# Two woven instruction streams in a two-layer hybrid encoder on eight cores

## The chip, the cores and the metric

The kernel runs on all 8 cores of one Trainium2 chip. Every core works alone on 4 of the 32 sequences. The metric is the device time of the slowest core, in microseconds.

The profiles name a core's engines: PE is the matmul array and PEld its weight loads, ACT computes activation functions, DVE and POOL work element by element, SP only issues transfers here. PSUM banks are the accumulators that matmuls write to and ACT and DVE read.

The chip has a second, slower state: in some executions the four cores of one die, or of both, run longer at a lower granted clock of the matmul array (PE). In a fast execution the granted clock is 1.00 or 0.50 and hardly anything else. In a slow one long stretches stand at 0.81: one slow die of the changed kernel had 6,955 us of them, a slow die of another version 15,086 us of 18,272. The die beside it may have none. So besides whole fast runs I compare **undisturbed dies**: the median span of the four cores of a die which shows the highest clock that this kernel reached. These medians repeat within 0.3%, across chips too. (The kernel before varies a little more: 18.10 to 18.19 ms.)

## The reference, cut to what matters

```python
# x: (32, 2048, 1024) float32; two layers; c modulates each norm per sequence
h = modulate(rms_norm(x, norm_ffn1[l]), sh1, sc1)
x = x + 0.5 * g1 * swiglu(h, ffn1_w_gu[l], ffn1_w_down[l])      # 1024 -> 2*2816 -> 1024
h = modulate(rms_norm(x, norm_mix[l]), sh2, sc2)
x = x + g2 * token_mix(h, ...)    # A: dense attention, 6 heads, rotary; B: window of +-128;
                                  # C: latent attention, 4 heads; gates, merge, projection
h = modulate(rms_norm(x, norm_ffn2[l]), sh3, sc3)
x = x + 0.5 * g3 * swiglu(h, ffn2_w_gu[l], ffn2_w_down[l])
# ... after the last layer: rms_norm(x, final_norm)
```

## The kernel before

One sequence at a time stays on the core (`xT`, four tiles of 512 tokens), and each sub-layer runs over all four tiles before the next begins. All engines follow one program; each works through its own instructions in order.

```python
def emit_norm_tile(l, m, s, tt):
    r, rres = emit_rstd(tt)     # squares on ACT, sums on PE, then Ln and Exp on ACT
    for c in range(KC):
        # DVE: tf = x * r          ACT: hT = tf * A + B
        ...

# ffn_steps(l, which, s): two groups of two tiles
for tg in range(2):
    for wt in range(NGU):
        add(gu_job(wt), gu_comp(wt, tg), tag=...)
        if tg == 1 and wt in (1, 3):
            add_next_norm(l, m, s, [wt // 2])   # next sub-layer's norm of a finished tile
    for dc in range(KC):
        add(dn_job(dc), dn_comp(dc, tg), tag=...)
add_next_norm(l, m, s, [2, 3])
# ... merge_steps: for tile tt, after its output projection:
if tt >= 1:
    add_next_norm(l, 1, s, [tt - 1])

# attn_dense: scores -> exp on ACT (one 512-column tile each) -> PV, one or two tiles ahead
for (g, tt, kc) in its:
    pend.append((g, tt, kc, emit_S(g, tt, kc)))
    if len(pend) > la:
        emit_PV(*pend.pop(0))
```

Eight PSUM banks serve whichever stage runs. Weights come straight from the fp32 inputs, and each block serves two tiles.

The softmax here doesn't subtract the row's maximum and nothing guards it: scores larger than these inputs give would overflow.

## Time and profile before

| | before |
|---|---|
| all timed runs | 18,189 (fast); 18,506; 18,621; 18,681 us |
| profiled execution | 18,161.6 us, cores 18,074 to 18,162, clock 0.90, at most 8.5 us at 0.81 |
| PE / ACT / DVE busy | 88% / 37% / 33% |

The page of the profile: busy time of each engine, the PE clock in tenths over 40 equal slices, the chain of waits, and the costliest group, FFN's gate and up matmuls (busy us in all, mean ns | idle before them, and what ended most of it).

```profile
span 18161.6 us, 218237 instructions; the slowest of 8 cores (18073.6 to 18161.6 us)
## 1 busy us (share of the span) xinstructions
PE 15968.4 (88%) x68808; PEld 6725.1 (37%) x68808; DVE 6000.9 (33%) x7933; ACT 6760.2 (37%) x12620; POOL 3347.6 (18%) x4221
...
PEclk9888999889898899888989889988998989999799
...
## 4 chain that ended last, share of the span: by engine, by line
PE 76%; ACT 8%; issue 6%; DVE 4%; DMA 3%; POOL 2%; ACTq 0%; DVEq 0%; POOLq 0%; SPq 0%
...
L468 PE MATMUL bank<-hT,wslot 128*128 128x512 bf16 x22528 | 5002.9, 385 | 153.2 <-ACT tmpf L473 153.2
```

The windows view of the same run, core 3 (busy us and, in brackets, instructions; then granted clock, DMA share, GB/s), for projections, dense attention, merge and FFN:

```profile
core 3: us, PE busy (x) PEld busy (x) DVE busy (x) ACT busy (x) POOL busy (x), PEclk, DMA share, GB/s
900.00:1000.00 100.00, 59.38 (x158) 18.91 (x156) 41.23 (x62) 35.59 (x58) 0.88 (x1) 0.69 0.08 19
1100.00:1200.00 100.00, 96.06 (x384) 27.47 (x384) 48.02 (x24) 98.78 (x193) 0.00 (x0) 1.00 0.00 1
1800.00:1900.00 100.00, 83.59 (x366) 35.81 (x365) 39.58 (x61) 29.80 (x47) 54.55 (x76) 0.95 1.32 124
4400.00:4800.00 400.00, 400.00 (x1855) 181.28 (x1853) 74.51 (x106) 50.46 (x86) 63.54 (x66) 1.00 0.68 75
```

FFN needs nothing but PE: 1,855 matmuls in 400 us at clock 1.00, 215.6 ns each. Dense attention runs at ACT's pace, 384 matmuls per 100 us. In projections PE waits and its clock falls.

### The profile page before, as it was taken

How to read it: one execution, taken by the hardware profiler on the slowest of the kernel's cores; microseconds unless marked ns; L12 is line 12 of the kernel's file. 1: busy time of each engine (PE TensorE's matmuls, PEld its weight loads, DVE VectorE, ACT ScalarE, POOL GpSimd, SP SyncE). 2: the span in 40 equal slices, each digit the busy share in tenths (PEclk: the TensorE clock that was granted, in tenths of full speed). 3: DMA queues.
4: the chain of work that ended last, by engine and by line, in shares of the span. 5: the costliest groups of instructions: out<-in, count | busy, mean ns of one | idle time of the engine just before them, and what ended most of it. 6: DMA issues, size and time to landing. Idle time of an engine off the chain costs nothing.

```text
span 18161.6 us, 218237 instructions; the slowest of 8 cores (18073.6 to 18161.6 us)
## 1 busy us (share of the span) xinstructions
PE 15968.4 (88%) x68808; PEld 6725.1 (37%) x68808; DVE 6000.9 (33%) x7933; ACT 6760.2 (37%) x12620; POOL 3347.6 (18%) x4221
## 2 busy tenths in 40 slices
PE   8988899878898899888988889988898888998799
PEld 5522444223442234323443234432344323443234
DVE  1144311443224432244222442234422344223442
ACT  1164211652216522264222642146312463225531
POOL 1111311113111131112201122111311113110141
PEclk9888999889898899888989889988998989999799
DMA  5603966129561295505855058630865409652195
GB/s 111 106 11 39 114 90 72 15 33 100 89 70 17 30 103 71 60 13 59 93 86 60 12 60 91 71 45 13 87 77 88 46 13 91 72 71 28 18 105 77
DMA packets 2876904, 1137.44 MB, mean 63 GB/s; under 512 B 2012566, under 2 KB 2816284, under 8 KB 2875804
## 3 DMA queue, kind: packets, MB, share of 16 engines
q0 software_dynamic: 2829952, 1004.51, 49.9%
q1 hardware_dynamic: 45852, 118.97, 2.0%
q8 instruction: 604, 9.90, 0.2%
q14 instruction: 496, 4.06, 0.1%
HBM read 2018.45 MB, written 33.56 MB: 113 GB/s over the span
## 4 chain that ended last, share of the span: by engine, by line
PE 76%; ACT 8%; issue 6%; DVE 4%; DMA 3%; POOL 2%; ACTq 0%; DVEq 0%; POOLq 0%; SPq 0%
PE bank L468 26%; PE bank L496 14%; PE bank L717 8%; PE bank L675 5%; PE bank L705 5%; PE bank L1050 5%; DMA wslot<-w_br_c 3%; PE bank L1080 2%; PE bank L316 2%; PE bank L1059 2%; PE bank L944 2%; ACT hT L412 2%; PE bank L396 1%; PE bank L885 1%; PE bank L867 1%
## 5 line engine op out<-in xcount | busy, mean ns | idle before, releaser
L468 PE MATMUL bank<-hT,wslot 128*128 128x512 bf16 x22528 | 5002.9, 385 | 153.2 <-ACT tmpf L473 153.2
L468 PEld LDWEIGHTS bank<-hT,wslot 128*128 128x128 bf16 x22528 | 2232.0, 99 | 2900.7 <-issue 333.8
L473 ACT ACTIVATE tmpf<-bank 128x512 f32<-128x512 f32 x1408 | 836.5, 597 | 5291.8 <-PE bank L468 5291.4
L709 ACT ACTIVATE pT<-bank 128x512 bf16<-128x512 f32 x5120 | 2611.8, 601 | 81.6 <-PE bank L705 39.6
L496 PE MATMUL bank<-scr,wslot 128*128 128x512 bf16 x11264 | 2479.1, 383 | 0.0
L475 DVE TENSOR_TENSOR scr<-tmpf,bank 128x512 bf16<-128x512 f32 x1408 | 964.5, 687 | 4021.0 <-PE bank L468 3824.0
L717 PE MATMUL bank<-pT,scr 128*128 128x512 bf16 x5120 | 1945.9, 386 | 62.0 <-ACT pT L709 5.6
L496 PEld LDWEIGHTS bank<-scr,wslot 128*128 128x128 bf16 x11264 | 1113.6, 99 | 1353.4 <-issue 54.1
L742 DVE RECIPROCAL tmpf<-bank 64x512 f32<-64x512 f32 x320 | 1072.5, 3352 | 1443.4 <-PE bank L717 1439.4
L1050 PE MATMUL bank<-hT,wslot 128*128 128x512 bf16 x6144 | 1402.7, 386 | 118.1 <-DMA wslot<-w_br_c 117.0
L705 PE MATMUL bank<-scr 64*128 64x512 bf16 (+1 forms) x5120 | 1410.5, 390 | 36.7 <-DVE tmpf L663 24.6
L454 POOL DMA_DIRECT2D wslot<-ffn_w_gu x704 | 615.1, 878 | 4430.7 <-PE bank L468 3448.5
L1033 POOL DMA_DIRECT2D wslot<-w_in x768 | 673.8, 886 | 3313.4 <-PE bank L997 2097.3
L675 PE MATMUL bank<-hT,wslot 128*128 128x512 bf16 x3584 | 1002.6, 443 | 295.1 <-DVE stg L959 123.0
L500 DVE SCALAR_TENSOR_TENSOR xT<-bank,modG,xT 128x512 f32<-128x512 f32 x512 | 384.4, 751 | 2156.8 <-PE bank L496 2156.8
L717 PEld LDWEIGHTS bank<-pT,scr 128*128 128x128 bf16 x5120 | 491.1, 96 | 1524.2 <-issue 1520.0
L1053 ACT ACTIVATE tmpf<-bank 128x512 f32<-128x512 f32 x768 | 454.4, 597 | 1488.5 <-PE bank L1050 976.8
L486 POOL DMA_DIRECT2D wslot<-ffn_w_down x512 | 541.8, 1063 | 2174.2 <-PE bank L496 1079.4
L1050 PEld LDWEIGHTS bank<-hT,wslot 128*128 128x128 bf16 x6144 | 603.9, 99 | 890.0 <-issue 212.7
L1063 DVE TENSOR_TENSOR tmpf<-tmpf,bank 128x512 f32<-128x512 f32 x768 | 493.6, 684 | 1096.8 <-ACT tmpf L1053 1053.9
L675 PEld LDWEIGHTS bank<-hT,wslot 128*128 128x128 bf16 x3584 | 381.3, 109 | 873.9 <-issue 580.3
L394 ACT ACTIVATE pT<-xT 128x512 bf16<-128x512 f32 x596 | 333.0, 618 | 954.8 <-PE bank L396 523.5
(128 smaller groups left out, 13239.0 us busy)
## 6 DMA issues: line engine op xcount, KB each, us to landing
wslot<-ffn_w_gu POOLq DMA_DIRECT2D x704, 512.0 KB, 7.8
wslot<-w_in POOLq DMA_DIRECT2D x800, 256.0 KB, 7.6
wslot<-ffn_w_down POOLq DMA_DIRECT2D x512, 352.0 KB, 6.6
wslot<-ada_w POOLq DMA_DIRECT2D x72, 1024.0 KB, 6.1
wslot<-w_out POOLq DMA_DIRECT2D x64, 1024.0 KB, 12.6
scr<-x SPq DMA_DIRECT2D x64, 512.0 KB, 3.9
scr<-ropeC SPq DMA_DIRECT2D x64, 512.0 KB, 3.9
out<-scr SPq DMA_DIRECT2D x64, 512.0 KB, 2.7
```

What stands on the lines that cost most here:

```text
L454: P.op("pool", lambda E, dst=dst, src=src: E.dma_start(out=dst, in_=src), writes=[res], chan=ch)
L468: P.op("pe", lambda E, bk=bk, g=g, k=k, half=half, tt=tt: E.matmul(bk[:], lhsT=W[:, k, g, half * 128:(half + 1) * 128], rhs=hT[:, k, tt * ...
L473: P.op("act", lambda E, tf=tf, pg=pg: E.activation(out=tf[:], in_=pg[:], func=AF.Silu), reads=[pgres], writes=[tres])
L475: P.op("dve", lambda E, tf=tf, pu=pu, f=f, t2=t2: E.tensor_tensor(out=act_view(f, t2), in0=tf[:], in1=pu[:], op=ALU.mult), reads=[tres, pu ...
L496: P.op("pe", lambda E, bk=bk, f=f, t2=t2: E.matmul(bk[:], lhsT=W[:, f, :], rhs=act_view(f, t2), start=(f == 0), stop=(f == FC - 1)), reads ...
L675: P.op("pe", lambda E, k=k: E.matmul(bk[0:M, :], lhsT=W[:, k, ncolchunk], rhs=hT[:, k, tt * TT:(tt + 1) * TT], start=(k == 0), stop=(k == ...
L705: P.op("pe", lambda E, sb=sb, ka=ka, qa=qa: E.matmul(sb[:], lhsT=ka, rhs=qa, start=True, stop=True), reads=[kres, qres], writes=[sbres])
L709: P.op("act", lambda E, sb=sb, pi=pi: E.activation(out=pT[pi][:], in_=sb[:], func=AF.Exp, scale=scale), reads=[sbres], writes=[pT_res[pi]])
L717: P.op("pe", lambda E, ob=ob, va=va, pi=pi: E.matmul(ob[:], lhsT=va, rhs=pT[pi][:], start=(kc == 0), stop=(kc == S // 128 - 1)), reads=[v_ ...
L742: P.op("dve", lambda E: E.reciprocal(out=tf[dlo:dlo + 64, 0:ncols], in_=ob[dlo:dlo + 64, 0:ncols]), reads=[obres], writes=[tres])
L1033: P.op("pool", lambda E, m=m, src=src: E.dma_start(out=G[:, m, :, :], in_=src), writes=[res], chan=ch)
L1050: P.op("pe", lambda E, bk=bk, m=m, k=k: E.matmul(bk[:], lhsT=G[:, m, k, :], rhs=hT[:, k, tt * TT:(tt + 1) * TT], start=(k == 0), stop=(k = ...
```

## The change

The intent: attention leaves PE waiting for ACT, FFN leaves ACT and DVE idle, so run them together, on different sequences. The program becomes two streams: F (norms, FFN, projections; q, k, v and h go to DRAM) and M (attention, gates, merge, output projection; the residual x comes from and goes to DRAM). A planner on the host weaves them into one order. F goes tile by tile: a tile of 512 tokens passes norm, FFN, norm, (FFN, norm,) projections, then the next tile starts. PSUM is split: two banks for F, six for M. Norms, SiLU and sigmoid are rewritten so that ACT keeps one table. The diff, cut to its core:

```diff
+LAT = 0.1; DMA_LAT = 2.0; DMA_RATE = 200e3; SLACK = 0.5     # one line each in the file
+def weave(streams):
+    # ... v: how far a stream is within its phase, by PE cost
+    # ... est(o): when o could start, from planned engine and buffer times
+    while True:
+        cands = []
+        for i, st in enumerate(streams):
+            o = st.ops[heads[i]]                # only the head of each stream's one list
+            if any(n not in toks for n in o.need):
+                continue
+            cands.append((est(o), i, o))
+        mn = min(c[0] for c in cands)
+        best = min((c for c in cands if c[0] <= mn + SLACK), key=lambda c: (c[2].v, c[0]))
+        # ... run(o): plan it, append it to the order
-    banks = [nc.alloc_psum_tensor("bank%d" % i, [128, TT], F32) for i in range(8)]
+    fbank = [nc.alloc_psum_tensor("fb%d" % i, [128, TT], F32) for i in range(2)]
+    sbk = [nc.alloc_psum_tensor("sb%d" % i, [128, 2 * TT], F32) for i in range(2)]
+    obk = [nc.alloc_psum_tensor("ob%d" % i, [128, TT], F32) for i in range(2)]
-        # ... rstd: two ACT operations, Ln and Exp
+    def rsqrt_rows(st, bk, br, nr, inv_n):      # eight DVE operations, [128, 512]
+        ts(st, ms, bk[0:nr, :], inv_n, EPS, ALU.mult, ALU.add, [br], [nr_r[0]])
+        ts(st, y.bitcast(I32), ms.bitcast(I32), -0.5, MAGIC, ALU.mult, ALU.add, ...)
+        for _ in range(2):
+            stt(st, t, y, -0.5, y, ALU.mult, ALU.mult, [nr_r[1]], [nr_r[2]])
+            tt_(st, "dve", t, t, ms, ALU.mult, [nr_r[2], nr_r[0]], [nr_r[2]])
+            stt(st, y, t, 1.5, y, ALU.add, ALU.mult, [nr_r[2], nr_r[1]], [nr_r[1]])
+    def norm(l, m, s):
+        norm_stats()
+        for c in range(KC):
+            t, tr = tmp()
+            tt_(F, "dve", t[:], xc(c), nr_y[:], ALU.mult, [xF_r[c], nr_r[1]], [tr])
+            act(F, hc(c), t[:], AF.Identity, ..., scale=mA(l, m, s, c), bias=mB(l, m, s, c))
+        # ... for every tile, in F's one list:
+            fsteps.append((ph, None, first(l - 1, 2, s)))
+            fsteps += ffn_steps(ph, l - 1, 1, s, tt, None)
+            fsteps.append((ph, None, lambda s=s, l=l: norm(l, 0, s)))
+            fsteps += ffn_steps(ph, l, 0, s, tt, 2 * l)
+            fsteps.append((ph, None, lambda s=s, l=l: norm(l, 1, s)))
+            fsteps += proj_steps(ph, l, s, tt, prefetch)
+    # ... weights: first touch in fp32, a bf16 copy is stored and reloaded for every tile
+    order, t_end, busy = weave([F, M])
```

## The prediction

> **What bounds the kernel now.** The array. In the profile (18162 us) the page's first part has PE busy 88% against DVE 33%, ACT 37%, POOL 18%; the chain of waits is 76% PE. But it is three different stages, seen in the windows view of one sequence and layer (about 2.2 ms). FFN: PE 100%, 465 matmuls per 100 us at granted clock 1.00 on all eight cores, so 215 ns per 512 columns. Dense attention: ACT 99%, PE issuing only 384 per 100 us (one 512-column exp each 0.51 us sets the pace). Projections and window attention: PE 57-83% busy at clocks 0.59-0.80, waiting for DVE and ACT in turn. Merge: PE 80-93%, DMA share up to 1.32 (rows under 512 B), waiting for the branch weights.
>
> I counted the matmul columns of both programs and priced them at 215 ns per 512 (fp32 four times), 64-row pairs as one. Before: 13.6 ms of pure array time, so 4.6 ms of its 18.16 ms are gaps, lowered clock (mean 0.90) and pipeline ends.
>
> **What changes.**
> - Removed: the second pass of C projections, 1024 input transposes in fp32, the zeroing matmuls, the 2304 four-column ada matmuls; window scores become 64-row pairs. New array time 13.0 ms: only 0.6 ms less. The pairs of A already overlap before (609 us for 3072).
> - Moved: attention and merge of one sequence run inside FFN, norms and projections of another. Per 512-token tile and layer: 406 us of array, against about 205 us of ACT and 215 us of DVE (durations of before: exp 0.51 us per 512, tanh 0.6, DVE op 0.69-0.75, reciprocal 3.35). No other engine binds on average, so the gaps are what can be won.
> - Added: DVE work (two ops per FFN chunk instead of one, rsqrt as eight DVE ops, about 0.8 ms) off the critical path; DMA. Weights are reread per tile, about 61 MB per 406 us, 150 GB/s instead of 63, but in 4 KB rows from bf16 copies. Loads of 512 KB landed in 3.9 us before; with 3 and 5 slots, about 7 to 14 us ahead, this hides.
> - No table switches: Silu, Sigmoid and Ln become tanh and DVE. The Trainium skill, "ScalarE: Activation LUTs", section on table sets, puts exp and tanh in one set; before shows loads of 1.28 us.
>
> **What is left of the gaps.** FFN has only two PSUM banks: its tanh (0.6) and first DVE op (0.75), plus latency, must fit under 1.72 us of the other bank's matmuls; behind a 1 us exp they don't. Estimate: 5-9% idle in woven stretches, 0.25 ms for the first and last phases (FFN alone, norms exposed), 0.25 ms first touch of fp32 weights, 0.1 ms start; clock about 0.98. Sum: 13.0/0.98/0.93 = 14.2, plus 0.6 = 14.8 ms. Timed runs of before are 2.5% over its profile; I allow part of it inside the range.
>
> **Predicted: 14800 us, range 13900 to 16000.** Faster by over 2%: 0.97; within: 0.02; slower: 0.01.
>
> **Right if** PE is over 92% busy with ACT and DVE near 50%; mean clock at least 0.96; almost no activation table loads; matmuls per 100 us near 420-450 throughout, without stage pattern; the chain of waits over 85% PE.
>
> **Wrong if** dense matmuls on eight cores trip a limiter: the Trainium skill, "TensorE: Matmul & The Clock Gate", HAM section, gives 13/16 clock for three busy cores; this trace doesn't agree (1.00 in FFN), but longer density could, giving about 16.5 ms. Or if the fixed order, in-order engines and two FFN banks stall PE on tanh behind exp (PE under 85%, waits on fb banks), or the single SP queue blocks weight loads behind stores (PE waiting for wF or wM).

## More of the kernel before

A "call" is a session in which several kernels were timed on one chip.

What PE waited for, before (total us, times, longest):

```profile
engine line waited for: us in total, times, longest us
PE bank L396 <- ACT pT L394: 198.8, 32, 10.5
PE bank L468 <- ACT tmpf L473: 153.2, 40, 4.8
...
PE bank L1050 <- DMA wslot<-w_br_c: 117.0, 77, 4.2
PE bank L396 <- ACT sq L394: 98.7, 16, 10.3
```

The two lines of L396 are the norms (statistics waiting for squares): some 300 us in 18 ms.

## The result, and the profile after

The changed kernel took 17,155 us in the median of four runs: 16,492 and 16,517 fast, 17,792 and 17,991 slow. The ratio of the fast runs is 0.908 (95% interval 0.905 to 0.911), 9% faster. Ratios are the mean time of one kernel's fast runs over that of the other's of the same rounds, so not quite the ratio of the medians quoted. The prediction said 14,800, and 13,900 to 16,000 as its range. The direction was right; the size was not.

The page of the profiled execution:

```profile
span 16515.5 us, 199324 instructions; the slowest of 8 cores (16449.4 to 16515.5 us)
...
PE 14310.3 (87%) x63128; PEld 5831.8 (35%) x63128; DVE 6429.4 (39%) x8558; ACT 5883.1 (36%) x7980; POOL 1591.9 (10%) x1365
...
PEclk8989998999999999999999999999999999999988
...
## 4 chain that ended last, share of the span: by engine, by line
PE 74%; DVE 9%; issue 6%; ACT 6%; DMA 3%; POOL 1%; SPq 1%; DVEq 0%; ACTq 0%; POOLq 0%
...
L510 PE MATMUL fb<-hF,wF 128*128 128x512 bf16 x25600 | 6927.5, 393 | 799.2 <-ACT hF L519 428.0
```

PE is busy 87%, not over 92; its clock is 0.93, not 0.96; the chain is 74% PE (76% before). Over the whole span 63,128 matmuls are 382 per 100 us, not 420 to 450. The windows view of core 7 shows that this is no even dilution: a stretch that is really woven, one in which attention runs alone, and one that holds a norm.

```profile
core 7: us, PE busy (x) PEld busy (x) DVE busy (x) ACT busy (x) POOL busy (x), PEclk, DMA share, GB/s
5780.00:5940.00 160.00, 159.20 (x757) 66.30 (x755) 52.15 (x60) 87.49 (x104) 5.08 (x4) 1.00 0.30 96
5400.00:5480.00 80.00, 67.21 (x299) 22.07 (x297) 20.99 (x15) 72.11 (x79) 5.06 (x4) 1.00 0.02 7
4945.00:4985.00 40.00, 26.54 (x117) 10.37 (x116) 25.84 (x34) 19.46 (x25) 1.79 (x1) 0.81 0.22 76
```

The woven stretch is what the change was made for: 757 matmuls in 160 us (473 per 100 us), PE busy 99.5%, clock 1.00, ACT at 55%. The losses lie elsewhere. What PE waited for, after:

```profile
engine line waited for: us in total, times, longest us
PE fb L510 <- ACT hF L519: 605.4, 163, 24.7
PE ob L510 <- DVE pT L522: 211.2, 101, 5.6
PE fb L510 <- DVE tmpf L522: 183.8, 76, 9.7
...
PE fb L510 <- DMA wF<-wts: 37.1, 20, 8.1
```

The largest entry, 605 us, is matmuls waiting for `hF`, which holds the squares and then the normalised tile; the norms' two lines of before came to some 300. In the group lines, the gate and up matmuls (with the projections, now) have 799 us of idle time before them, 428 of it ended by `hF`; before, gate and up had 153. The other 177 of the 605 us are statistics waiting for squares. All matmul waits for weight DMA are short (37 us for the first-touch loads), though DMA moves 142 GB/s instead of 63.

One norm in the timeline of core 7 (start us, us, engine, line, operation, tiles, and in brackets the idle time before it):

```profile
start us, us, engine line op out<-in xcount [idle before <-releaser]
4962.53 0.69 DVE L533 TENSOR_SCALAR nr<-fb 128x512 f32<-128x512 f32 x1
...
4965.47 1.49 DVE L526 SCALAR_TENSOR_TENSOR nr<-nr 128x512 f32<-128x512 f32 x2
...
4968.65 4.91 DVE L522 TENSOR_TENSOR tmpf<-xF,nr 128x512 f32<-128x512 f32 x8
4969.44 5.77 ACT L519 ACTIVATE hF<-tmpf,mods,modA 128x512 bf16<-128x512 f32 x8 [8.00 <-DVE tmpf L522]
...
4970.40 4.12 PE L510 MATMUL fb<-hF,wF 128*128 128x512 bf16 x6 [8.40 <-ACT hF L519]
...
4973.47 3.35 DVE L1121 RECIPROCAL mt<-mt 128x512 f32<-128x512 f32 x1
...
4974.46 0.61 PE L510 MATMUL sb<-q,kB 64*128 64x384 bf16 x4
```

The root occupies DVE from 4962.53 to 4968.6, then the eight multiplications go to ACT one by one, and PE starts at 4970.40, 8.4 us idle, at first with one matmul per 0.7 us. M does not fill the hole: its next score matmul comes at 4974.46, and its reciprocal had to stand behind the norm's DVE operations until 4973.47. The Trainium skill, "TensorE: Matmul & The Clock Gate", section on architectural detail, says that ACT and DVE are strict first-in first-out queues; this timeline agrees. The clock in 5-us steps around the same norm:

```profile
core 7: us, PE busy (x) PEld busy (x) DVE busy (x) ACT busy (x) POOL busy (x), PEclk, DMA share, GB/s
4955.00:4960.00 5.00, 5.00 (x27) 1.94 (x25) 2.07 (x4) 3.28 (x4) 0.00 (x0) 1.00 0.51 173
...
4965.00:4970.00 5.00, 0.00 (x0) 0.00 (x0) 4.47 (x8) 0.56 (x1) 0.00 (x0) 0.50 0.00 0
4970.00:4975.00 5.00, 3.99 (x11) 0.76 (x11) 5.00 (x7) 5.00 (x8) 0.00 (x0) 0.50 0.01 2
4975.00:4980.00 5.00, 4.44 (x24) 1.81 (x22) 4.54 (x4) 2.81 (x4) 1.79 (x1) 0.86 0.09 17
```

The gap halves PE's clock, and the first matmuls after it run at half speed. The skill's same page ("What's actually happening") says an idle array falls to half clock after an idle window of about 3.4 us and recovers after a busy one. The trace agrees: its stretches of 0.50 are 3.41 us or multiples of it (but for those that the end of the span cuts), 13.65 us at this norm. In all, core 1 of after stood 2,254 of its 16,451 us at 0.50.

From the records of the traces, a span can be split into three terms: PE's busy time weighed with the granted clock (**work**), the rest of its busy time (**clock**), and its idle time. On cores without a stretch at 0.81 (sums are short by 5 to 15 us, because idle time after the last matmul is left out; the stretch before the first clock record, 168 us in before and 31 in after, is counted at 0.50, since fp32 matmuls of 128 columns start 213 ns apart there, and 109 ns apart where a record says 1.00):

| | span | work | clock | idle |
|---|---|---|---|---|
| before, core 5 | 18,150 | 14,586 | 1,378 | 2,180 |
| after, core 1 | 16,451 | 13,624 | 663 | 2,149 |
| the prediction's sum | 14,800 | 13,000 | 270 | about 1,600 |

(13.0/0.98 gives the clock term, dividing by 0.93 gives 1.0 ms of idle time, and the 0.6 ms of phases and start are counted as idle.) So the whole gain of 1.7 ms is less work, 1.0, and better clock, 0.7. **The idle time did not shrink at all**, although it is this that the weave was meant to remove. On core 7 of the profile, where every matmul record is there, 1,093 of the 2,191 us of idle time lie inside 112 norm windows (from the first statistics matmul to the eighth of F's weight matmuls after it, cut where the next window begins), 10 us each, and all windows but one hold 3 us or more. (The expectations below quote 1.24 ms from a first count; with overlaps of the windows counted twice it is 1.22.) Another 389 lie in 50 stretches of over 8 us in which only attention matmuls run.

### The profile page after: what moved, and what is told of

It reads as the page before. It is cut to its first block, busy times and chain, and to the rows that moved or that the text cites. A ratio compares the mean times of both kernels' runs of the same rounds, so it can differ in the third digit from the quotient of the medians.

```text
span 16515.5 us, 199324 instructions; the slowest of 8 cores (16449.4 to 16515.5 us)
## 1 busy us (share of the span) xinstructions
PE 14310.3 (87%) x63128; PEld 5831.8 (35%) x63128; DVE 6429.4 (39%) x8558; ACT 5883.1 (36%) x7980; POOL 1591.9 (10%) x1365
## 4 chain that ended last, share of the span: by engine, by line
PE 74%; DVE 9%; issue 6%; ACT 6%; DMA 3%; POOL 1%; SPq 1%; DVEq 0%; ACTq 0%; POOLq 0%
PE fb L510 53%; PE sb L510 12%; PE ob L510 9%; ACT pT L519 3%; DVE nr L526 2%; DVE pT L522 1%; DVE tmpf L522 1%; ACT hF L519 1%; DVE mt L1121 1%; DVE nr L522 1%; ACT mt L519 1%; DVE nr L533 1%; DMA mt<-xs 1%; SPq L543 1%; POOL tmpf L522 1%
## 5 line engine op out<-in xcount | busy, mean ns | idle before, releaser
L510 PE MATMUL fb<-hF,wF 128*128 128x512 bf16 x25600 | 6927.5, 393 | 799.2 <-ACT hF L519 428.0
L510 PEld LDWEIGHTS fb<-hF,wF 128*128 128x128 bf16 x25600 | 2478.2, 100 | 4395.3 <-issue 1877.2
L510 PE MATMUL fb<-actb,wF 128*128 128x512 bf16 x11520 | 3042.3, 383 | 50.2 <-DMA wF<-wts 17.3
L519 ACT ACTIVATE pT<-sb 128x1024 bf16<-128x1024 f32 x2560 | 2514.8, 1024 | 1293.3 <-PE sb L510 1278.9
L510 PE MATMUL ob<-pT,vv 128*128 128x512 bf16 x6176 | 1855.0, 372 | 468.0 <-DVE pT L522 211.2
L526 DVE SCALAR_TENSOR_TENSOR tmpf<-tmpf,fb 128x512 f32<-128x512 f32 x1408 | 965.8, 686 | 2727.2 <-ACT tmpf L519 2598.0
L510 PEld LDWEIGHTS fb<-actb,wF 128*128 128x128 bf16 x11520 | 1117.7, 98 | 1485.1 <-issue 210.1
L522 DVE TENSOR_TENSOR actb<-tmpf,fb 128x512 bf16<-128x512 f32 x1536 | 1056.1, 688 | 1258.8 <-PE fb L510 1034.9
L510 PE MATMUL sb<-hM,wM 128*128 128x512 bf16 x4160 | 1297.1, 388 | 30.1 <-DMA wM<-wts_bf 30.1
L1121 DVE RECIPROCAL mt<-mt 128x512 f32<-128x512 f32 x256 | 857.9, 3351 | 46.2 <-ACT mt L519 34.6
```

Source lines behind the costliest of these rows:

```text
L510: st.op("pe", lambda E: E.matmul(out, lhsT=lhsT, rhs=rhs, start=start, stop=stop, skip_group_check=True), reads=reads, writes=writes, cost ...
L519: st.op("act", lambda E: E.activation(out=out, in_=in_, func=func, **kw), reads=reads, writes=writes, cost=c_act(n))
L522: st.op(eng, lambda E: E.tensor_tensor(out=out, in0=a, in1=b, op=op), reads=reads, writes=writes, cost=c_dve(n) if eng == "dve" else c_poo ...
L526: st.op("dve", lambda E: E.scalar_tensor_tensor(out=out, in0=a, scalar=scalar, in1=b, op0=op0, op1=op1), reads=reads, writes=writes, cost= ...
L1121: M.op("dve", lambda E: E.reciprocal(out=den, in_=den), reads=[denr], writes=[denr], cost=c_rec(TT))
```

## The experiments

Theory N: the missing 1.7 ms are exposed norms, 7 per tile and 112 in all, with their idle time and the half clock behind it. Before, they hid among other tiles' matmuls. Rivals: W, the weave itself (one list for each stream, only its head a candidate, planned with assumed rates), which runs attention alone at ACT's pace; and D, the DMA traffic of 2,346 MB instead of 1,137. Times below are undisturbed dies unless another state is named; the kernel after is 16.47 ms in the same terms, and before 18.10 to 18.19.

### unwoven

```diff
-        best = min((c for c in cands if c[0] <= mn + SLACK), key=lambda c: (c[2].v, c[0]))
+        best = min(cands, key=lambda c: (c[2].phase, c[1]))    # each phase: all of F, then all of M
```

> The changed kernel with one thing undone: the two streams are not interleaved; of each phase the FFN stream is placed whole, then the attention and merge stream. Same instructions. If weaving is what the change gives (theory A), this loses all of the 1.65 ms gain and more, because norms and attention stand bare and stay in the two-bank layout: 18.3 to 19.3 ms in the fast state. If most of the gain is the smaller work (rival: fewer matmul columns, no transposes, no table switches), it stays near 17 ms.

Correct. No whole run was fast (19,580 to 20,342 us); its best dies took 18,592 to 18,609 us at clock 0.89 in four runs, inside theory A's range. Weaving is worth 2.1 ms: without it the same operations are slower than the kernel before (18,158 to 18,191 us). The rewriting alone (tiles, tanh, DRAM, split banks) gains nothing in this order.

### norm_one_op

```diff
         ms, y, t = nr_ms[0:nr, :], nr_y[0:nr, :], nr_t[0:nr, :]
+        if nr == 128:       # wrong on purpose: one operation for the eight of the root
+            ts(st, y, bk[0:nr, :], 0.0, 1.0, ALU.mult, ALU.add, [br], [nr_r[1]])
+            return
```

> Wrong output on purpose: the reciprocal root of the 128-row norms is one vector instruction in place of eight in a row. Theory N (the 112 norms are where the array idles: 1.24 of 2.19 ms idle and about 0.8 of 1.17 ms of lost clock lie in or just behind them): the chain is 5 us shorter, 112 x 5 us = 0.56 ms of idle and about half as much clock loss go, 15.6 to 15.9 ms. Rival B (FFN's two banks, tanh behind a 1 us exp) and rival P (attention run alone at ACT pace): at most 0.2 ms.

Wrong as intended (relative error 0.043). 16.01 to 16.02 ms, one whole run fast at 16,035: 0.46 ms gained, short of theory N's range by 0.1. Idle time on core 5 is 1,731 us, of it 557 in the norm windows. Seven DVE operations fewer, 5 us a norm, gave this, and the two rivals allowed 0.2. The norms matter, but the root is not all of them.

### slack0

```diff
-SLACK = 0.5
+SLACK = 0.0
```

> One constant of the scheduler: it may no longer let a stream that lags behind go first when that stalls the engine by up to 0.5 us; 0 in its place. Same instructions, other order. Theory P (attention alone for 1.13 ms at ACT pace, idle 0.39 ms in it, comes of this rule): 0.3 to 0.5 ms faster, 16.0 to 16.2 ms, and the stretches of attention alone shrink to under half. If they are there for want of ready FFN work: under 0.1 ms.

Correct, 15.90 to 15.92 ms. With slack, the planner may put the stream that lags first although its operation can start up to 0.5 us later; on an in-order queue that is a hole. Removing it gave 0.57 ms, but not where I looked for it: stretches of attention alone keep 1,103 us (1,134 after) and their idle time rises from 389 to 490 us. The norm windows keep 1,021 us of idle time. What shrank is the holes elsewhere. So the gain came out a little above the range, and the reason given for it did not hold.

### ooo

```diff
 def weave(streams):
-    # candidates: the head of each stream's list
+    # each stream has a queue per engine; the head of each queue is a candidate as soon as
+    # the ops before it that share a buffer with it are placed
+            for e, qq in q.items():
+                n, o = qq[0]
+                g = group(qq) if o.glue else [qq[0]]
+                if any(x not in done and x not in mine for _, m in g for x in deps[m]):
+                    continue
+                cands.append((est(o), o.v, i, e, len(g)))
-SLACK = 0.5
-DMA_RATE = 200e3
+SLACK = 0.0
+PE_LAT = 0.15
+DMA_RATE = 320e3
```

> Another scheduler, same instructions: each engine takes its own next instruction of a stream once those it shares a buffer with are placed, so a vector instruction at the head of the attention stream no longer keeps its later matmuls behind the norm; slack 0; DMA assumed at 320 GB/s in place of 200. If the norm's gaps are for want of placed work (theory N, second half), 15.2 to 15.7 ms, PE idle in norm windows at most half; if vector work itself is short there (rival D), at least 15.9 ms like slack0.

Correct, 15.46 to 15.48 ms, one whole run fast at 15,504: 1.0 ms less than after with the same instructions. Idle time is 1,460 us; stretches of attention alone fall to 797 us. A norm window still idles 7.5 us (844 in all), more than the half that theory N allowed. So W is a real term, as large as norm_gone will show N to be. This version changed the plan's assumptions too; list_320 separates the two.

### list_320

```diff
-DMA_RATE = 200e3
-SLACK = 0.5
+DMA_RATE = 320e3
+SLACK = 0.0
```

> Correct. The weave of the changed kernel with its slack at 0 and its assumed DMA rate at 320 instead of 200 GB/s; a stream stays one list. Separates the two things that the out-of-order version changed. If one list per stream is what costs: within 1% of slack0, 15.8-15.95 ms on an undisturbed die. If the pessimistic DMA rate in the plan is what costs: 15.4-15.6 ms, as the out-of-order version.

Correct, 15.74 to 15.75 ms. Neither expectation held: the assumed DMA rate is worth 0.16 ms and the lists the remaining 0.28. So the 1.0 ms of the planner splits into 0.57 for the slack, 0.16 for the rate, and 0.28 for one list for each stream, the last with the small changes of assumed latencies in it.

### norm_gone and ooo_norm_gone

```diff
-        act(F, hc(c), xc(c), AF.Square, [xF_r[c]], [hF_r[c]])
+        act(F, hc(c), xc(c), AF.Tanh, [xF_r[c]], [hF_r[c]])     # wrong on purpose, bounded
-        rsqrt_rows(F, bk, br, 128, 1.0 / D)
+        ts(F, nr_y[:], bk[:], 0.0, 1.0, ALU.mult, ALU.add, [br], [nr_r[1]])
     def norm(l, m, s):
         norm_stats()
-        for c in range(KC):
-            ...                 # eight multiplications on DVE, eight scalings on ACT
```

> Wrong on purpose: of each of the 112 norms only the statistics' matmuls and one DVE operation stay; the rest of the root chain (7 operations), the eight multiplications and the eight scalings are not done, and the matmuls read a bounded function of x that ACT writes where it wrote the squares. The weave is the one of the changed kernel. Theory N (the missing term is the exposed norms, idle and the clock behind it): an undisturbed die goes from 16.45-16.5 ms to 14.9-15.5 ms, PE's idle time from 2.19 ms to about 1.2 ms, mean clock from 0.93 to 0.95 or more. Rival W (the loss is in the weave, which runs attention alone at ACT's pace whatever F does): 16.0 ms or more, and the idle time only moves.

Wrong as intended (0.21). 15.50 to 15.52 ms on the better die in three runs, one whole run fast at 15,653: 0.95 ms gained, just past the upper end of theory N's range. The clock rose to 0.96 as N said, but 1,519 us of idle time stay, more than N's 1.2 ms. What PE still waits for (core 5):

```profile
engine line waited for: us in total, times, longest us
PE ob L510 <- DVE pT L522: 217.2, 104, 5.8
...
PE fb L510 <- ACT hF L519: 138.2, 54, 18.8
```

The wait for `hF` is down from 605 us on core 7 (586 on core 5) to 138 (statistics waiting for ACT's writes are among them); the waits of attention's exp and of window attention's DVE products stay. N is over half of what is missing, not all.

> Wrong on purpose, as norm_gone, with the out-of-order plan. If norms and the one-list weave are the two terms that the prediction left out, the prediction's 14.8 ms must be reached or beaten here: 14.2-14.8 ms on an undisturbed die, PE's idle time under 1.0 ms, clock 0.97 or more. If it stays over 15 ms, a third term is missing.

With the other planner and without norms: 14.74 ms, one whole run fast at 14,782. N and W held. This is the prediction's 14.8 ms, at idle time 982 us and clock 0.972; but it is a kernel that leaves work out, and its terms are not the prediction's (work 13.48 ms, not 13.0; idle 0.98, not about 1.6). That the sums meet so closely is luck; what the run shows is that the two terms are large enough. The two gains (0.95 and 1.0) overlap by 0.2. The view of all cores of its profiled run shows how a slow and an undisturbed die stand side by side:

```profile
die 0 (median of its cores): 15172.2 us, clock 0.932
die 1 (median of its cores): 14742.3 us, clock 0.972
```

### ooo_cols, cols

```diff
     def norm_stats():
         for c in range(KC):
-            mm(F, bk[:], ONE, hc(c), c == 0, c == KC - 1, ...)
+            for g in range(4):      # tokens on the partitions: sums land in [128, 4]
+                mm(F, bk[:, g:g + 1], hF[:, c * TT + g * 128:c * TT + (g + 1) * 128], ONE[:, 0:1], ..., n=1)
-        rsqrt_rows(F, bk, br, 128, 1.0 / D)
+        # the same eight DVE operations on [128, 4], split into two bf16 parts, then
+        for g in range(4):
+            for hl in range(2):     # spread over the partitions again
+                mm(F, b2[:, g * 128:(g + 1) * 128], nhl[:, hl * 4 + g:hl * 4 + g + 1].to_broadcast([128, 128]), IDB, ..., n=128)
```

> Correct. The out-of-order plan, and the norm's statistics with tokens on the partitions: 32 matmuls of one column, the eight operations of the root on 128x4 instead of 128x512, then eight matmuls of 128 columns that spread the result. Theory N: the chain from statistics to the first scaled chunk shrinks by about 3.5 us of 11, 112 times, and what it gives back is idle time at half clock: 15.1-15.3 ms on an undisturbed die (15.47 before this). Rival W: within 0.5% of 15.47 ms.

Correct, 15.32 to 15.33 ms, one whole run fast at 15,347: 0.9% faster than ooo, between the two expectations. With the better planner the root itself is worth 0.14 ms.

> Correct. The plan of the changed kernel (slack 0.5, one list for each stream), with the norm's root on 128x4 as in ooo_cols. The version with one operation in place of eight saved 0.46 ms; this one keeps all eight, small, and adds a spreading matmul: 16.0-16.25 ms on an undisturbed die. Within 0.5% of 16.47 if only the scaling operations and not the root matter.

Correct, in the changed kernel's own plan: 16.25 ms on its two undisturbed dies, 0.22 ms gained, at the weak end of the range.

### norm_not_awaited

```diff
-            mm(F, bk[:], ONE, hc(c), c == 0, c == KC - 1, [hF_r[c], const_r], [br])
+            mm(F, bk[:], ONE, hZ[:], c == 0, c == KC - 1, [const_r], [br])      # hZ: constant tile
-                    mm(F, pg[:], W[:, k, 0, :], hc(k), k == 0, k == KC - 1, [sr, hF_r[k]], [pgr])
+                    mm(F, pg[:], W[:, k, 0, :], hZ[:], k == 0, k == KC - 1, [sr, const_r], [pgr])
# the same for pu and for the A, B and C projections; every operation of the norm stays
```

> Wrong on purpose: all work of the norms is done, at the same places of the plan, but the matmuls that used its result (statistics, gate and up, A, B and C projections) read a constant tile instead. If the latency of the norm's result is the cost: 15.5-15.7 ms on an undisturbed die, as when the norms are gone. If the cost is their place in the lists and queues (the FFN's first tanh and the other stream's operations stand behind their 24 operations on ACT and DVE): 16.2 ms or more, and PE's idle time stays over 1.9 ms. I expect the second.

Wrong as intended (0.63). 16.33 to 16.34 ms on three undisturbed dies: only 0.13 ms gained, and idle time on core 5 is 2,220 us, no less than after. "The same places of the plan" holds inside F's list; the planner, which no longer sees these waits, merges M a little otherwise (58,087 of the 63,128 matmuls stand at the same place of PE's order). What PE waits for now:

```profile
engine line waited for: us in total, times, longest us
PE fb L511 <- DVE tmpf L527: 440.8, 121, 21.0
PE ob L511 <- DVE pT L523: 271.3, 105, 12.9
PE fb L511 <- ACT actb L520: 262.6, 110, 10.7
```

The 605 us that had the name `hF` moved to another name: 441 us for the FFN's first DVE operation `tmpf<-tmpf,fb`, which with the product after it frees F's two banks, 121 waits, and 263 us for ACT operations on `actb`. The page's releaser was true, and yet removing it gained almost nothing, because the FFN's own tanh and products follow the norm's 24 ACT and DVE operations in F's list and in the queues. Together with norm_gone (the same waits gone and the operations too: 0.95 ms) this shows that a norm costs by the operations that stand ahead, which wait for each other, and not by the matmuls' own wait for its result. How much of that is the order in F's list and how much the queues of ACT and DVE is not separated, and it is shown for the plan of the changed kernel only.

### half_loads

```diff
+            nl[0] += 1
+            m = n if nl[0] < 500 else n // 2      # wrong on purpose
-            dma(st, sl[:, 0:n], wb_d[l * NWJ + i][:, 0:n], [r], [res], ch, 128 * n * 2)
+            dma(st, sl[:, 0:m], wb_d[l * NWJ + i][:, 0:m], [r], [res], ch, 128 * n * 2)
```

> Wrong on purpose: the order of the changed kernel, but after the first 500 reloads of a weight block only half of its columns are fetched, which takes about a quarter of all bytes away. If the doubled DMA traffic (142 GB/s) is what ate the gain: 16.0 ms or less on an undisturbed die. If it is hidden, as the short DMA waits of PE say (about 0.15 ms in all): 16.35-16.5 ms.

Wrong as intended (0.29). The core moved 1,726 MB instead of 2,346, and took 16.445 ms in three runs, against 16.47 of the changed kernel (undisturbed dies). PE's order is that of after, matmul by matmul. D falls: the traffic is hidden.

### exp_quarter

```diff
-                    act(M, pT[p][:], sbk[i][:], AF.Exp, ..., n=1024, scale=A_SCALE)
+                    act(M, pT[p][:, 0:256], sbk[i][:, 0:256], AF.Exp, ..., n=256, scale=A_SCALE)   # wrong on purpose; C too
```

> Wrong on purpose: each exp of dense attention takes 256 of its 1024 columns, about 0.4 us in place of 1.02, 2560 times; the plan knows it. Removes ACT's pace from attention while the norms stay. Rival W (attention alone at ACT's pace, 0.39 ms of idle time): about 16.0 ms on an undisturbed die. Theory N (norms, which hold F's side whatever attention costs): at least 16.2 ms, and the idle time around the norms stays at 1.1-1.3 ms.

Wrong as intended (0.024). Two undisturbed dies, 16.128 and 16.133 ms: 0.34 ms gained, between the two expectations, so ACT's pace is a third and smaller term. (The shorter exps also leave ACT sooner to F's tanh and scalings; the run doesn't separate that.)

### after_again and best

after_again is the changed kernel, untouched.

> The changed kernel, untouched, on the same chip as the other runs of this call, so that a fast run or an undisturbed die of it stands beside theirs: 16.45-16.5 ms, clock 0.93.

16.466 to 16.475 ms on four undisturbed dies, as expected.

best is ooo_cols with M's residual tiles loaded one step earlier, and 0.25 us for the latency behind PE in the plan:

```diff
-PE_LAT = 0.15
+PE_LAT = 0.25
             def wo(q, tt=tt, hold=hold, xload=xload):
                 def fn(sl, sr):
-                    # allocate and load this step's two residual tiles
+                    xs = hold.pop(("xs", q))
+                    if q < 3:
+                        xload(q + 1, tt, hold)      # q = 0: loaded at the end of the gates
```

> Correct. The out-of-order plan, the norm's root on 128x4, and the residual tiles of the output projection loaded one step earlier (their loads take 6.6 us to land and stand in the chain of waits of the out-of-order version). 15.15-15.35 ms on an undisturbed die (15.33 without the early loads); PE's idle time no more than 1.33 ms, and the share of the residual's load in the chain of waits gone.

Correct, 15.27 to 15.30 ms, one whole run fast at 15,284. It is within its range. The residual's load did not leave the chain (1%, 2% in ooo). Its page:

```profile
span 15282.6 us, 205343 instructions; the slowest of 8 cores (15253.6 to 15282.6 us)
...
PE 13858.8 (91%) x65430; PEld 5900.6 (39%) x66712; DVE 5999.7 (39%) x8782; ACT 5863.0 (38%) x7980; POOL 1593.6 (10%) x1365
...
PEclk8999999999999999999999999999999999999998
...
PE 76%; DMA 6%; issue 5%; ACT 5%; DVE 5%; SPq 2%; POOL 1%; DVEq 0%; ACTq 0%; POOLq 0%
```

best beats both kernels: on undisturbed dies 15.27/16.47 = 0.93 of the changed kernel in the same call, and 0.84 of some 18.15 of the kernel before in other calls. Its two edits were not run apart, and the 0.05 ms that they gain on ooo_cols is no more than 0.4%.

| undisturbed die | ms | work | clock | idle (us) |
|---|---|---|---|---|
| before | 18.15 | 14,586 | 1,378 | 2,180 |
| after | 16.47 | 13,624 | 663 | 2,149 |
| norm_not_awaited (core 5, 295 us at 0.81) | 16.34 | 13,556 | 598 | 2,220 |
| norm_one_op | 16.01 | 13,652 | 602 | 1,731 |
| slack0 | 15.90 | 13,544 | 542 | 1,801 |
| list_320 | 15.74 | 13,530 | 499 | 1,709 |
| norm_gone | 15.52 | 13,594 | 401 | 1,519 |
| ooo | 15.46 | 13,548 | 480 | 1,460 |
| best | 15.27 | 13,478 | 479 | 1,291 |
| ooo_norm_gone | 14.74 | 13,478 | 255 | 982 |

The times are medians of a die, the three terms those of one of its cores in the profiled execution, so they sum to about that core's span. From after on work hardly moves; the clock term goes down with the idle time, without any edit that aims at the clock.

## Why the prediction was right or wrong

- **Faster, and by the mechanism of filling gaps of one stage with another's matmuls: right.** In the woven stretch shown, PE is 99.5% busy at clock 1.00, and unwoven costs 2.1 ms.
- **The step that failed: "Estimate: 5-9% idle in woven stretches, 0.25 ms for the first and last phases (FFN alone, norms exposed) ...; clock about 0.98."** Idle time was 2.15 ms, 13% of the span, against about 1.6 summed; the clock cost 0.66 ms of PE's busy time against 0.27. (Term by term the sum missed by about 0.55 ms of idle time, 0.4 of clock, and 0.6 of work; the next point is about the last.) The estimate was taken from the balance of engines over a whole tile ("no other engine binds on average") and looked only at the FFN's steady loop. It put exposed norms into the first and last phases alone. The trace shows 3 us or more of idle time at 111 of the 112 norms: the change walks one tile through its sub-layers, so a norm has no other tile's matmuls around it in F, and in the timeline M does not fill in, with its operations on DVE behind the norm's. That the walk of one tile is to blame is read from this order; no run put another tile's matmuls around a norm again. The better planner alone doesn't cure the gaps: a norm window of ooo still idles 7.5 us. Taking the norms away gave 0.95 ms, the better planner 1.0 ms, both together 1.73 ms, as much as the missing 1.7. A third, smaller term is ACT's pace (0.34 ms; how much of it lies inside the planner's 1.0 was not run).
- **"New array time 13.0 ms": counted right, used wrongly.** Work was 13.62 ms. I had counted 13.6 for before, where the same measure gives 14.6, and had noted "pipeline ends" there, but gave after none. Of the 0.62 ms too little, some 0.35 are ends: 2,747 matmuls stand before a gap and count 343 ns each instead of 215. The Trainium skill, "Perfetto Trace Analysis", section on tensor engine instructions, says the profiler estimates a matmul's end, which no run here can check; so this part of work is modelled and not measured, and it shrinks with the gaps (1,344 such matmuls in ooo_norm_gone). Most of the other 0.27 stands in the trace of after (core 1): where matmuls follow each other without a gap at clock 1.00, they take 0.25 ms more than the price of their columns, about half of it at the score matmuls on 64 rows. The two of a pair start 4 ns apart, but a full matmul is followed by a pair after 312 ns, and a pair by a full matmul after 318, where two full ones start 216 ns apart. The columns themselves come to 12.94 ms in the trace, at 215 ns per 512 and twice that for fp32, as measured (429 ns). With the 0.35 and the 0.25 that makes 13.54 of the 13.62 ms.
- **DMA hides: right.** Loads of 512 KB landed in 3.8 us (F) and 4.3 (M); half_loads gained 0.15%.
- **Almost no table loads: right.** 131 before, 1 after, 1,283 ns each.
- **DVE and ACT near 50%, chain over 85% PE, 420 to 450 matmuls per 100 us throughout: wrong**, 39%, 36%, 74% and 382, with the very stage pattern that was to vanish. All follow for the most part from the longer span: per tile and layer ACT was busy 184 us (205 expected) and DVE 201 (215).
- **"Wrong if ... a limiter ... giving about 16.5 ms": the number came out, the cause did not.** In the fast profile PE ran at 1.00 in the woven stretch shown, and core 7 spent 157 us at 0.81, core 1 none. (The "1.00 on all eight cores" for FFN before is 0.96 to 1.00 in the windows view, the rest being stretches of 0.50.) The limiter is the slow state.
- **"Or if the fixed order, in-order engines and two FFN banks stall PE": the right worry, given too little weight.** Its sign, waits on the F banks, was there; PE stalled on the norm's operations more than on tanh behind exp. PE was 87% busy, not under 85.
- **"Timed runs of before are 2.5% over its profile; I allow part of it"**: this was the slow state, not a cost.

## What to carry to other kernels

Balance over a whole tile is no bound for an in-order machine: look for serial chains (norms, roots, softmax ends), count them, and ask what other work stands ahead of and behind each in the queues; a restructuring that removes one kind of gap may bring hidden chains into the open. A wait names the last releaser, not the cost: remove that one wait, keep the work, and see whether the time moves before believing it. And when two streams are merged by a plan, the planner is part of the kernel: letting each engine take the next ready operation, taking no slack and assuming faster transfers was, all together, worth as much as deleting every norm.

## What the Trainium skill lacked or had wrong

- "TensorE: Matmul & The Clock Gate" says that a die falls to 13/16 of the clock soon after a third core starts dense matmuls, and holds it. The records agree with the ratio (0.812) but not with the condition: in the profile of before eight cores ran FFN for 400 us on end without a stretch at 0.81 (clock 0.96 to 1.00), whole executions of the changed kernel had none of it on a core, and others had 6,955 us (after_again) or 15,086 us (exp_quarter) of it, one die apart from the other. The page should say that it comes and goes between executions of the same program and is what makes a run slow.
- No page of those on the vector engine that I read gives the time of a reciprocal on DVE: 3.35 us for 512 columns in these traces, five times the 0.69 us of a multiplication.
